# One decoder layer: the rests of every second weight piece on GpSimd until the MLP, the convolution as a side job, and new constants in the layout's clock

## The chip, the cores and the metric

The kernel runs on one core of a Trainium2 chip. The engines of the core are named as in the profile: PE (TensorE, matrix products; PEld its weight loads), DVE (VectorE), ACT (ScalarE), POOL (GpSimd) and SP (SyncE, which here issues the larger loads). The metric is the device time of the whole program in microseconds (us), as the median of several runs.

## What is computed

One inference step of one layer: 256 prompt tokens and 8 x 8 sample tokens (320 columns together), model width 2048, all in fp32. Cut to what matters:

```python
z = rmsnorm(x, g_mix) @ w_in            # 2048 x 3584: B, C, H, q, k, v, qx
y_conv = b * short_conv(c * hc, conv_w) # 3 taps along the sequence, width 512
y_swa  = sink_attention(q, k, v, ...)   # 8 heads, window 128, biases from a table
y_x    = cross_attention(qx, mk, mv)    # 4 heads, mk and mv from mem @ w_mem_k, w_mem_v
x = x + concat(y_conv, y_swa, y_x) @ w_out
x = x + square(relu(rmsnorm(x, g_mlp) @ w_up)) @ w_down   # width 8192
...
def short_conv(u_ext, w):
    length = u_ext.shape[1] - (CONV_K - 1)
    out = w[0] * u_ext[:, 0:length]
    for i in range(1, CONV_K):
        out = out + w[i] * u_ext[:, i:i + length]
    return out
```

The sample tokens attend to caches of their own (window keys and values, memory keys and values), and the new keys, values and convolution states are outputs too.

## The kernel before

**Weights.** All weight matrices are cut into 360 *pieces* of 256 x 512, 512 KB each. SP loads a piece into one of four buffers `raw`. `split_piece` then makes two halves of it in one of four buffers: ACT rounds it to fp32r (`wh`), and the *rest*, `wl = raw - wh`, is left to `rest()`, which issues the subtraction on DVE and then calls `load_piece()`: the load of the piece four places on goes into the `raw` buffer that the rest has just read. In SP's row of instructions that load waits for the rest, and everything behind it on SP waits too. The split of piece i is put out once PE has used piece i - 4. Each product is three fp32r matmuls (high by high, high by low, low by high).

**Groups and steps.** Pieces are used in this order: cross queries (0 to 7), K and V (8 to 15), w_mem_k (16 to 23), w_mem_v (24 to 31), Q (32 to 47), C (48 to 55), H (56 to 63), B (64 to 71), w_out (72 to 103), then the MLP (104 to 359). A *step* is one call of `run_unit`: 12 matmuls of 320 columns, half a piece, or 6 of 512 columns in the two memory groups. At its end `boundary()` puts out, in this order, late evacuations, evacuations (`h_evac` multiplies H by C and does the convolution; `b_evac` multiplies the convolution by B), the rests, and one step of the side jobs.

**Side jobs.** Norms, both attentions, the position biases and the convolution's state run as generators in `Side`: each is resumed at a boundary, puts out a few instructions and yields. When a job goes on is decided while the program is built, by a clock of its own, `Pace`: it adds up a cost for each operation on each engine (`cost`, `load`), and `after(...)` yields until by that clock the tiles are written. `LAG` is the landing time that it gives to loads other than weights. The order in which instructions stand in each engine's row thus follows from these numbers; on the chip each engine takes its row in order and waits on semaphores. `cross_sample` loads the cached memory keys (`cmk`) and values (`cmv`) into buffers `w`, two of a batch at a time and two batches ahead; `swa_sample` does the same with the cached window keys and values (`csk`, `csv`). `bias_sample_job` fetches the sample biases with eight small loads (`z<-sk_d`) from POOL's queue. `pre_late` copies the old window keys and values from one place of memory to another, also from POOL's queue (`old_k`, `old_v`), at the turn from B to w_out.

**Names and lines in the profile.** Nearly every operation is recorded at line 166, the wrapper in `Paced`. Weight products are `mm<-...`, those of the side jobs `ax<-...`. The convolution works on `lx` (H times C with its earlier columns) into `z`, 128 x 336.

Of the kernel before, what the change touches and what calls it, by code (L numbers as in the profile page):

```python
# [9 lines left out]
F32 = mybir.dt.float32  # L10
F32R = mybir.dt.float32r
AF = mybir.ActivationFunctionType
ALU = mybir.AluOpType
# [18 lines left out]
NEG = -1e30  # L32

NW2 = 12
LAG = 6.0
WARM = 10
C_B, C_C, C_H, C_Q, C_K, C_V, C_X = 0, 512, 1024, 1536, 2560, 2816, 3072


# [53 lines left out]
class Pace:  # L93
# [12 lines left out]
    def cost(self, eng, op, out, ins):  # L106
        n = max(a.free_size() for a in [out] + ins)
        if eng == "pe":
            n = out.free_size()
            if ins[0].dtype == F32R:  # L110
                return 0.0033 + n / 2400.0
            quarter = 0.25 if out.partition_size() == 32 else 1.0
            return 0.0009 * n if op == "transpose" else max(0.11, n / 600.0) * quarter
        if eng == "act":
            return 0.1 + n * 0.00083
        if eng == "dve":
            return 0.08 + n * 0.00104
        return 0.1 + n * 0.0025

    def issue(self, eng, op, out, ins):  # L120
# [13 lines left out]

    def load(self, out):
        start = max(self.clock["dma"], self.clock["pe"])
        self.clock["dma"] = start + out.free_size() * 4 * out.partition_size() / 330e3
        self.wrote[out.name] = (self.clock["dma"] + (2.0 if out.name.startswith("raw") else LAG), "dma")

    def ready(self, tiles):  # L140
# [6 lines left out]
class Paced:  # L147
# [3 lines left out]
    def __getattr__(self, op):  # L151
        f = getattr(self.engine, op)
        if not callable(f) or op == "preload_act_table_set":
            return f

        def issue(*args, **kw):
            aps = [a for a in list(kw.values()) + list(args) if isinstance(a, bass.AP)]
            out = kw["out"] if "out" in kw else args[0]
            if op == "dma_start":
                if out.name not in self.pace.dram:  # L160
                    self.pace.load(out)
            else:
                if "accum_out" in kw:
                    self.pace.wrote[kw["accum_out"].name] = (self.pace.clock[self.name] + 0.5, self.name)
                self.pace.issue(self.name, op, out, [a for a in aps if a is not out])
            return f(*args, **kw)  # L166

        return issue
# [79 lines left out]
def trunk_step(ctx: ExitStack, tc: tile.TileContext, I, O):  # L248
    nc = tc.nc
    pace = Pace()  # L250
    side = Side(NW2, pace)
    pace.dram = {a.name for a in list(I.values()) + list(O.values())}
    pe, act, dve = (Paced(pace, n, e) for n, e in (("pe", nc.tensor), ("act", nc.scalar), ("dve", nc.vector)))
    pool, sp = Paced(pace, "pool", nc.gpsimd), Paced(pace, "dma", nc.sync)
# [14 lines left out]
    zs = Slots(zp, "z", 10)  # L269
# [16 lines left out]
    def zt(cols=336):  # L286
        return zs.need([P, 336])
# [43 lines left out]
    def gcol(name, i=0):  # L331
        return cols[:, col[name] + i:col[name] + i + 1]
# [6 lines left out]
    st = {}  # L339
# [62 lines left out]
    def load_piece():  # L402
        i = count["load"]
        if i >= len(pieces):
            return
        count["load"] += 1
        wt[i] = raw_p.tile([P, 2, 512], F32, name="raw", tag="raw")
        if i > 1:
            load_part(i, slice(0, 2))
# [5 lines left out]
    def split_piece():  # L415
        i = count["split"]
        if i >= len(pieces) or (i >= SPL and done_at.get(i - SPL, count["unit"]) >= count["unit"]):
            return
        count["split"] += 1
        pace.clock["act"] = max(pace.clock["act"], pe_done.get(i - SPL, 0.0))  # L420
        r = wt.pop(i)
        h = wsp.tile([P, 2, 512], F32R, name="wh", tag="wh")
        l = wsp.tile([P, 2, 512], F32R, name="wl", tag="wl")
        wt[i] = (h, l)
        if i < 2:

            for c in range(2):
                k = 2 * i + c
                x = xblk[0][:, k, :]
                if k:  # L430
                    split_act(S0h[:, k, :], S0l[:, k, :], x, gcol("g_mix", k))
                else:
                    dve.tensor_scalar(out=S0h[:, k, :], in0=x, scalar1=gcol("g_mix", k), scalar2=None, op0=ALU.mult)
                    dve.scalar_tensor_tensor(out=S0l[:, k, :], in0=x, scalar=gcol("g_mix", k),
                                             in1=S0h[:, k, :].bitcast(F32), op0=ALU.mult, op1=ALU.subtract)
                act.activation(out=h[:, c, :], in_=r[:, c, :], func=AF.Copy)
                dve.tensor_tensor(out=l[:, c, :], in0=r[:, c, :], in1=h[:, c, :].bitcast(F32), op=ALU.subtract)
            side.flags.add(f"x{i}")
            load_piece()
            return  # L440
        act.activation(out=h, in_=r, func=AF.Copy)

        def rest():
            dve.tensor_tensor(out=l, in0=r, in1=h.bitcast(F32), op=ALU.subtract)
            load_piece()

        subs.append(rest)

    def add_group(w, c0, korder, a, evac, kind="std", needs=None, pre=None, k0=0):
# [36 lines left out]
    def run_unit(un):  # L486
# [6 lines left out]
        while count["split"] <= un["base"] + un["ps"][-1]:  # L493
            split_piece()
# [43 lines left out]
        if u == 2 * un["n"] - 1 or u % 2 and len(un["ps"]) == 1 or u == 3:  # L538
            for i in un["ps"]:
                done_at[un["base"] + i] = count["unit"]  # L540
                pe_done[un["base"] + i] = pace.clock["pe"]
        count["unit"] += 1
        split_piece()
        boundary()

# [13 lines left out]
    def split_act(hi, lo, src, gain):  # L559
        act.activation(out=hi, in_=src, func=AF.Copy, scale=gain)  # L560
        dve.scalar_tensor_tensor(out=lo, in0=src, scalar=gain, in1=hi.bitcast(F32), op0=ALU.mult, op1=ALU.subtract)
# [567 lines left out]
    def usample(m):  # L1129
        return st["u"][:, m, 258:UC].rearrange("p (b r) -> p b r", r=10)  # L1130

    def per_batch(a):
        return a.rearrange("p (b t) -> p b t", t=NS)
# [19 lines left out]
    def h_evac(m, ps):  # L1153
        if m == 0:
            st["y"] = {}
        u = st["u"]
        z = zs.must([P, 336])
        dve.tensor_tensor(out=z[:, 0:T], in0=ps, in1=rb, op=ALU.mult)
        dve.tensor_tensor(out=u[:, m, 2:258], in0=z[:, 0:TP], in1=u[:, m, 2:258], op=ALU.mult)
        us = usample(m)[:, :, 2:10]  # L1160
        dve.tensor_tensor(out=us, in0=per_batch(z[:, TP:T]), in1=us, op=ALU.mult)
        dve.tensor_scalar(out=z, in0=u[:, m, 0:336], scalar1=gcol("conv_w", m), scalar2=None, op0=ALU.mult)
        for i in (1, 2):
            dve.scalar_tensor_tensor(out=z, in0=u[:, m, i:i + 336], scalar=gcol("conv_w", 4 * i + m), in1=z,
                                     op0=ALU.mult, op1=ALU.add)
        st["y"][m] = z
        if m == 3:
            side.add("convout", conv_out_job())

    def conv_out_job():  # L1170
        cu = yield from zt()
        u = st["u"]
        for m in range(4):
            dve.tensor_copy(out=cu[:, m * 18:m * 18 + 2], in_=u[:, m, 256:258])
            dve.tensor_copy(out=cu[:, m * 18 + 2:m * 18 + 18].rearrange("p (b r) -> p b r", r=2),
                            in_=u[:, m, 258:UC].rearrange("p (b r) -> p b r", r=10)[:, :, 8:10])
        pool.dma_start(out=O["conv"], in_=cu[:, 0:72])
        zs.put(cu)
        lx.put(st.pop("u"))
        yield 1  # L1180

    def b_evac(m, ps):
        side.until(["cp"])
        y = st["y"][m]
        z = zs.must([P, 336])
        dve.tensor_tensor(out=z[:, 0:T], in0=ps, in1=rb, op=ALU.mult)
        dve.tensor_tensor(out=z[:, 0:TP], in0=z[:, 0:TP], in1=y[:, 0:TP], op=ALU.mult)
        dve.tensor_tensor(out=z[:, TP:T].rearrange("p (b t) -> p b t", t=NS),
                          in0=z[:, TP:T].rearrange("p (b t) -> p b t", t=NS),
                          in1=y[:, 256:336].rearrange("p (b r) -> p b r", r=10)[:, :, 2:10], op=ALU.mult)  # L1190
        act.activation(out=S1h[:, m, :], in_=z[:, 0:T], func=AF.Copy)
        zs.put(y)

        def rest():
            dve.tensor_tensor(out=S1l[:, m, :], in0=z[:, 0:T], in1=S1h[:, m, :].bitcast(F32), op=ALU.subtract)
            zs.put(z)

        later.append(rest)
        if m == 3:
            side.flags.add("conv")  # L1200
# [92 lines left out]
    add_group(w_in, C_Q + 512, order, xa, q_evac(4))  # L1293
    add_group(w_in, C_C, order, xa, c_evac)
    add_group(w_in, C_H, order, xa, h_evac)
    add_group(w_in, C_B, order, xa, b_evac)

    for g in range(4):
# [30 lines left out]
    bk = ax.must([P, 512])  # L1329
    for _ in range(WARM):  # L1330
        nc.tensor.matmul(out=bk[:, 0:P], lhsT=ones, rhs=ones, start=True, stop=True)
# [72 lines left out]
```

## Time and profile before

| | us |
|---|---|
| median of 3 runs (1320.54 to 1321.83) | 1320.77 |
| the profiled execution | 1322.82 |
| its span | 1320.7 |
| PE busy | 1311.3 |
| DVE busy | 674.7 |
| ACT busy | 541.3 |
| POOL busy | 18.1 |

The profiled execution's own time holds 2.1 us beside the span that the trace covers. POOL issues a few loads and fills a few tiles; a load that it issues counts as about half a microsecond of its time. The mean clock granted to PE is 0.997 of full speed. In the rows of a timeline the first column is the start, the second the duration in us, and a bracket holds the idle time just before the instruction and what ended it.

### The profile page before, as it was taken

What the parts mean: (1) busy time and instruction counts of PE and PEld (TensorE: products, weight loads), DVE (VectorE), ACT (ScalarE), POOL (GpSimd) and SP (SyncE); (2) the same over time, 40 slices, a digit from 0 to 9 for tenths busy, and PEclk for the clock granted to TensorE, in tenths of its full rate; (3) what the DMA queues carried; (4) which work ended last, traced back from release to release, by engine and by line L of the source; (5) the groups of instructions that cost most, each with busy time, mean ns of one, the idle gap of its engine ahead of it and who ended that gap; (6) DMA issues with size and microseconds to landing.
All of it is one profiled execution on the core that took longest, in us unless ns stands there. A gap on an engine that the chain in (4) does not pass through costs nothing.

```text
span 1320.7 us, 21556 instructions
## 1 busy us (share of the span) xinstructions
PE 1311.3 (99%) x8956; PEld 1289.5 (98%) x8956; DVE 674.7 (51%) x1025; ACT 541.3 (41%) x801; POOL 18.1 (1%) x37
## 2 busy tenths in 40 slices
PE   9999999999999999999999999999999999999999
PEld 9988999889999999999999999999999999999998
DVE  6877665766566444443344543434444344444343
ACT  7684563334355444332334433234442223443321
POOL 1011000000000000000000000000000000000000
PEclk9999999989999999999999999999999999999999
DMA  8668454456344444445444445444444444444552
GB/s 313 236 200 286 167 188 159 178 184 228 108 153 159 148 157 144 144 144 160 156 148 144 141 149 166 151 145 142 147 159 158 144 153 135 155 153 155 171 172 72
DMA packets 65489, 217.03 MB, mean 164 GB/s; under 512 B 8438, under 2 KB 10718, under 8 KB 65361
## 3 DMA queue, kind: packets, MB, share of 16 engines
q1 hardware_dynamic: 63184, 210.14, 48.1%
q0 software_dynamic: 1776, 5.26, 1.1%
q8 instruction: 70, 1.15, 0.4%
q10 hardware_dynamic: 432, 0.28, 0.1%
q14 instruction: 27, 0.21, 0.0%
HBM read 211.53 MB, written 7.65 MB: 166 GB/s over the span
## 4 chain that ended last, share of the span: by engine, by line
PE 93%; DVE 3%; DMA 2%; ACT 1%; issue 1%; SPq 0%; DVEq 0%; ACTq 0%
PE mm L166 90%; PE ax L166 3%; DMA raw<-in_w_in 2%; DVE z L166 1%; DVE wl L166 1%; ACT wh L166 1%; DVE lx L166 0%; ACT lx L166 0%; DVE S1l L166 0%; DVE w L166 0%; DVE sm L166 0%; ACT z L166 0%; ACT S0h L166 0%; DVE S0l L166 0%; ACT S1h L166 0%
## 5 line engine op out<-in xcount | busy, mean ns | idle before, releaser
L166 DVE TENSOR_TENSOR wl<-raw,wh 128x1024 fp32r<-128x1024 f32 (+1 forms) x362 | 436.1, 1217 | 487.3 <-ACT wh L166 476.4
L166 ACT ACTIVATE wh<-raw 128x1024 fp32r<-128x1024 f32 (+1 forms) x362 | 374.5, 1050 | 629.1 <-PE mm L166 581.1
L166 PE MATMUL mm<-S0h,wh 128*128 128x320 f32 x1472 | 455.8, 311 | 0.8 <-DVE z L166 0.4
L166 PE MATMUL mm<-S0h,wl 128*128 128x320 f32 x1472 | 453.6, 310 | 1.1 <-DVE wl L166 1.1
L166 PE MATMUL mm<-S0l,wh 128*128 128x320 f32 x1472 | 453.7, 310 | 0.3 <-DVE S0l L166 0.3
L166 PE MATMUL mm<-S1h,wh 128*128 128x320 f32 x1280 | 397.4, 310 | 0.0
L166 PE MATMUL mm<-S1h,wl 128*128 128x320 f32 x1280 | 395.5, 309 | 0.0
L166 PE MATMUL mm<-S1l,wh 128*128 128x320 f32 x1280 | 395.5, 309 | 0.0
L166 PEld LDWEIGHTS mm<-S0h,wh 128*128 128x128 f32 x1472 | 276.5, 188 | 3.3 <-issue 1.4
L166 PEld LDWEIGHTS mm<-S0h,wl 128*128 128x128 f32 x1472 | 276.6, 188 | 1.3 <-DVE wl L166 1.3
L166 PEld LDWEIGHTS mm<-S0l,wh 128*128 128x128 f32 x1472 | 276.7, 188 | 0.6 <-DVE S0l L166 0.6
L166 PEld LDWEIGHTS mm<-S1h,wh 128*128 128x128 f32 x1280 | 240.4, 188 | 0.2
L166 PEld LDWEIGHTS mm<-S1l,wh 128*128 128x128 f32 x1280 | 240.4, 188 | 0.2
L166 PEld LDWEIGHTS mm<-S1h,wl 128*128 128x128 f32 x1280 | 240.3, 188 | 0.0
L166 DVE TENSOR_TENSOR lx<-mm,lx 128x320 f32<-128x320 f32 (+1 forms) x97 | 46.8, 485 | 77.1 <-PE mm L166 77.0
L166 ACT ACTIVATE z<-z 128x320 f32<-128x320 f32 (+1 forms) x118 | 55.0, 470 | 64.4 <-DVE z L166 63.2
L166 DVE TENSOR_TENSOR S1l<-z,S1h 128x320 fp32r<-128x320 f32 x68 | 33.4, 491 | 51.1 <-ACT S1h L166 51.1
L166 ACT ACTIVATE S1h<-z 128x320 fp32r<-128x320 f32 x68 | 32.1, 472 | 7.5 <-DVE z L166 5.5
L166 DVE SCALAR_TENSOR_TENSOR z<-mm,r2b 128x320 f32<-128x320 f32 x64 | 31.0, 484 | 0.0
L166 PE MATMUL mm<-wh,S1h 128*128 128x512 f32 x64 | 25.6, 400 | 0.0
L166 PE MATMUL mm<-wl,S1h 128*128 128x512 f32 x64 | 25.0, 391 | 0.0
L166 PE MATMUL mm<-wh,S1l 128*128 128x512 f32 x64 | 25.0, 391 | 0.0
(162 smaller groups left out, 432.5 us busy)
## 6 DMA issues: line engine op xcount, KB each, us to landing
raw<-in_w_up SPq DMA_DIRECT2D x128, 512.0 KB, 3.3
raw<-in_w_down SPq DMA_DIRECT2D x128, 512.0 KB, 3.3
raw<-in_w_in SPq DMA_DIRECT2D x54, 512.0 KB, 4.1
raw<-in_w_out SPq DMA_DIRECT2D x32, 512.0 KB, 3.7
raw<-in_w_mem_k SPq DMA_DIRECT2D x8, 512.0 KB, 6.4
raw<-in_w_mem_v SPq DMA_DIRECT2D x8, 512.0 KB, 4.3
w<-in_cmk SPq DMA_DIRECT2D x16, 256.0 KB, 5.8
w<-in_cmv SPq DMA_DIRECT2D x16, 256.0 KB, 5.1
```

The costliest lines, as they stand in the source:

```text
L166: return f(*args, **kw)
```

## The change

Three things. First, the rests of the odd pieces from 9 to 103, 48 in all, are subtracted on POOL instead of DVE; the load behind each then waits for POOL. Second, the three operations of the convolution leave `h_evac`, which gives its buffer back; a new side job `convy` does them one tile every two steps, and adds the job of the convolution's state at its end; `b_evac` is held until `convy` is done. Third, the constants of the build-time clock are others: each operation on ACT and DVE costs 0.1 and 0.08 more, a matmul 0.01 more, loads flow at 410 instead of 330 KB per us, `LAG` is 3.5 instead of 6.0, and an operation with an accumulated output takes longer. From piece 104 on the order of all engines is as it was.

```diff
@@ -32,8 +32,9 @@
 NEG = -1e30
 
 NW2 = 12
-LAG = 6.0
+LAG = 3.5
 WARM = 10
+POOLED = 8, 104
 C_B, C_C, C_H, C_Q, C_K, C_V, C_X = 0, 512, 1024, 1536, 2560, 2816, 3072
 
 
@@ -108,13 +109,13 @@
         if eng == "pe":
             n = out.free_size()
             if ins[0].dtype == F32R:
-                return 0.0033 + n / 2400.0
+                return 0.0135 + n / 2400.0
             quarter = 0.25 if out.partition_size() == 32 else 1.0
             return 0.0009 * n if op == "transpose" else max(0.11, n / 600.0) * quarter
         if eng == "act":
-            return 0.1 + n * 0.00083
+            return 0.2 + n * 0.00084
         if eng == "dve":
-            return 0.08 + n * 0.00104
+            return 0.16 + n * 0.00105
         return 0.1 + n * 0.0025
 
     def issue(self, eng, op, out, ins):
@@ -134,7 +135,7 @@
 
     def load(self, out):
         start = max(self.clock["dma"], self.clock["pe"])
-        self.clock["dma"] = start + out.free_size() * 4 * out.partition_size() / 330e3
+        self.clock["dma"] = start + out.free_size() * 4 * out.partition_size() / 410e3
         self.wrote[out.name] = (self.clock["dma"] + (2.0 if out.name.startswith("raw") else LAG), "dma")
 
     def ready(self, tiles):
@@ -161,8 +162,10 @@
                     self.pace.load(out)
             else:
                 if "accum_out" in kw:
-                    self.pace.wrote[kw["accum_out"].name] = (self.pace.clock[self.name] + 0.5, self.name)
+                    self.pace.wrote[kw["accum_out"].name] = (self.pace.clock[self.name] + 0.9, self.name)
                 self.pace.issue(self.name, op, out, [a for a in aps if a is not out])
+                if "accum_out" in kw:
+                    self.pace.clock[self.name] += 0.19
             return f(*args, **kw)
 
         return issue
@@ -440,8 +443,10 @@
             return
         act.activation(out=h, in_=r, func=AF.Copy)
 
+        eng = pool if i % 2 and POOLED[0] <= i < POOLED[1] else dve
+
         def rest():
-            dve.tensor_tensor(out=l, in0=r, in1=h.bitcast(F32), op=ALU.subtract)
+            eng.tensor_tensor(out=l, in0=r, in1=h.bitcast(F32), op=ALU.subtract)
             load_piece()
 
         subs.append(rest)
@@ -1159,13 +1164,21 @@
         dve.tensor_tensor(out=u[:, m, 2:258], in0=z[:, 0:TP], in1=u[:, m, 2:258], op=ALU.mult)
         us = usample(m)[:, :, 2:10]
         dve.tensor_tensor(out=us, in0=per_batch(z[:, TP:T]), in1=us, op=ALU.mult)
-        dve.tensor_scalar(out=z, in0=u[:, m, 0:336], scalar1=gcol("conv_w", m), scalar2=None, op0=ALU.mult)
-        for i in (1, 2):
-            dve.scalar_tensor_tensor(out=z, in0=u[:, m, i:i + 336], scalar=gcol("conv_w", 4 * i + m), in1=z,
-                                     op0=ALU.mult, op1=ALU.add)
-        st["y"][m] = z
+        zs.put(z)
         if m == 3:
-            side.add("convout", conv_out_job())
+            side.add("convy", conv_job())
+
+    def conv_job():
+        u = st["u"]
+        for m in range(4):
+            z = yield from zt()
+            dve.tensor_scalar(out=z, in0=u[:, m, 0:336], scalar1=gcol("conv_w", m), scalar2=None, op0=ALU.mult)
+            for i in (1, 2):
+                dve.scalar_tensor_tensor(out=z, in0=u[:, m, i:i + 336], scalar=gcol("conv_w", 4 * i + m), in1=z,
+                                         op0=ALU.mult, op1=ALU.add)
+            st["y"][m] = z
+            yield 2
+        side.add("convout", conv_out_job())
 
     def conv_out_job():
         cu = yield from zt()
@@ -1180,7 +1193,7 @@
         yield 1
 
     def b_evac(m, ps):
-        side.until(["cp"])
+        side.until(["cp", "convy"])
         y = st["y"][m]
         z = zs.must([P, 336])
         dve.tensor_tensor(out=z[:, 0:T], in0=ps, in1=rb, op=ALU.mult)
```

The first place is the end of group H in DVE's row, before: the evacuations of tiles 1, 2 and 3 (`z<-mm,rb` is an H tile scaled from PE's sums, `lx` its product with C, the last two rows of each the convolution), with the sample attention's softmax between.

```order
L166 TENSOR_TENSOR z_2893<-mm,rb 128x320
L166 TENSOR_TENSOR lx_1381<-z_2893,lx_1381 128x256
L166 TENSOR_TENSOR lx_1381<-z_2893,lx_1381 128x8x8
L166 TENSOR_SCALAR z_2893<-lx_1381,cols 128x336
L166 SCALAR_TENSOR_TENSOR z_2893<-lx_1381,cols,z_2893 128x336 x2
L166 TENSOR_TENSOR z_2918<-mm,rb 128x320
L166 TENSOR_TENSOR lx_1381<-z_2918,lx_1381 128x256
L166 TENSOR_TENSOR lx_1381<-z_2918,lx_1381 128x8x8
L166 TENSOR_SCALAR z_2918<-lx_1381,cols 128x336
L166 SCALAR_TENSOR_TENSOR z_2918<-lx_1381,cols,z_2918 128x336 x2
```

The same place in DVE's row now, from tile 2 of H to the first convolved tile, past the turn to group B:

```order
L169 TENSOR_TENSOR z_3029<-mm,rb 128x320
L169 TENSOR_TENSOR lx_1384<-z_3029,lx_1384 128x256
L169 TENSOR_TENSOR lx_1384<-z_3029,lx_1384 128x8x8
L169 TENSOR_TENSOR z_3052<-mm,rb 128x320
L169 TENSOR_TENSOR lx_1384<-z_3052,lx_1384 128x256
L169 TENSOR_TENSOR lx_1384<-z_3052,lx_1384 128x8x8
L169 TENSOR_TENSOR wl<-raw,wh 128x1024
L169 TENSOR_SCALAR z_3059<-lx_1384,cols 128x336
L169 SCALAR_TENSOR_TENSOR z_3059<-lx_1384,cols,z_3059 128x336 x2
```

The convolution's rows stand behind the last H evacuation and a rest, one tile at a time.

The second place is POOL's row from the start to the sample biases, before (`gkx` a gain vector; `rv_d`, `sk_d` position biases on their way through memory):

```order
L166 DMA gkx<-in_g_k_x 128x128
L166 MEMSET w_5_441 128x512
L166 MEMSET w_6_442 128x512
L166 DMA rv_d<-w_12_539 8x384
L166 DMA sk_d<-rv_d 1024x1x384
L166 DMA z_1093<-sk_d 8x136 x8
```

And now:

```order
L169 DMA gkx<-in_g_k_x 128x128
L169 ISA
L169 TENSOR_TENSOR wl<-raw,wh 128x1024 [waits DMAHW4_49,PE_49,Activation_49]
L169 MEMSET w_6_455 128x512
L169 MEMSET w_7_456 128x512
L169 DMA rv_d<-w_9_461 8x384 [waits Activation_49]
L169 DMA sk_d<-rv_d 1024x1x384 [waits DMASW6_49]
```

The `ISA` row reloads POOL's library of instructions; the first rest, that of piece 9, follows it. Seven more rests follow behind these rows, and then the eight bias loads with rests right behind them.

The third place is SP's row around the first cached keys of the cross attention (group w_mem_k), before, with the semaphores that each waits for (`DVE_49`: the rest):

```order
L166 DMA raw<-in_w_mem_v 128x1024 [waits DMAHW5_49,DVE_49]
L166 DMA w_17_1090<-in_c_own 128x2x64
L166 DMA w_17_1090<-in_c_rep 32x128
L166 DMA w_18_1102<-in_cmk 128x512
L166 DMA w_19_1104<-in_cmk 128x512
L166 DMA w_20_1106<-in_cmk 128x512 [waits DMAHW6_49]
L166 DMA w_21_1108<-in_cmk 128x512 [waits DMAHW7_49]
```

And now:

```order
L169 DMA w_17_1037<-in_c_own 128x2x64
L169 DMA w_17_1037<-in_c_rep 32x128
L169 DMA raw<-in_w_mem_v 128x1024 [waits DMAHW4_49,Pool_49]
L169 DMA w_18_1079<-in_cmk 128x512
L169 DMA w_19_1081<-in_cmk 128x512
L169 DMA w_20_1083<-in_cmk 128x512 [waits DMAHW5_49]
L169 DMA w_21_1085<-in_cmk 128x512 [waits DMAHW6_49]
```

A weight load has come between the two small loads and the keys, and it waits for a rest on POOL. The keys are put out five steps ahead of their first use, the bias loads on POOL seven. At the first cached window keys (group C) it is the same now:

```order
L169 DMA raw<-in_w_in 128x1024 [waits DMAHW7_49,DMAHW3_49,Pool_49]
L169 DMA w_71_2541<-in_csk 128x512 [waits DMAHW4_49,PE_49]
L169 DMA w_72_2543<-in_csv 128x512 [waits DMAHW5_49,PE_49]
L169 DMA w_73_2545<-in_csk 128x512 [waits PE_49]
```

Before, the weight load ahead of `csk` there waited for DVE (`[waits DMAHW6_49,DMAHW2_49,DVE_49]`). The use of the first key stands four steps behind its load now.

## Prediction

> **What bounds the kernel now.** I read the busy table and the slices first, for which engine fills the span, then the chain, the waits and one stretch in windows of 5 us.
>
> ```profile
> PE 1311.3 (99%) x8956; PEld 1289.5 (98%) x8956; DVE 674.7 (51%) x1025; ACT 541.3 (41%) x801; POOL 18.1 (1%) x37
> PEclk9999999989999999999999999999999999999999
> PE 93%; DVE 3%; DMA 2%; ACT 1%; issue 1%; SPq 0%; DVEq 0%; ACTq 0%
> 423.36 894.08 PE mm L166 x6096
> ```
>
> PE is busy 99% of the span and carries 93% of the chain. From 423 us on the chain is nothing but matmuls, 894.08 / 6096 = 0.1467 us each, 3.52 us for a piece's 24. The order is unchanged from the MLP on (piece 104) and the matmuls are the same ones, so nothing can come from there. What is to be had is PE's idle time and lost clock ahead of 423 us. The list of waits gives the first:
>
> ```profile
> PE ax L166 <- DVE z L166: 2.6, 2, 1.9
> PE mm L166 <- DVE wl L166: 1.1, 1, 1.1
> PE mm L166 <- DVE z L166: 0.4, 1, 0.4
> PE ax L166 <- ACT z L166: 0.2, 1, 0.2
> ```
>
> These are sums, counts and longest waits. PE's timeline puts them in place, the wait in brackets:
>
> ```profile
> 39.42 0.41 PE L166 MATMUL ax<-z,mean_d 128*128 128x320 f32 x1 [0.17 <-ACT z L166]
> 40.48 0.42 PE L166 MATMUL ax<-z,mean_d 128*128 128x320 f32 x1 [0.64 <-DVE z L166]
> 256.68 0.41 PE L166 MATMUL mm<-S0h,wh 128*128 128x320 f32 x1 [0.45 <-DVE z L166]
> 260.05 0.42 PE L166 MATMUL mm<-S0h,wl 128*128 128x320 f32 x1 [1.06 <-DVE wl L166]
> 274.98 0.79 PE L166 MATMUL ax<-vns,z 64*128 64x128 f32 x2 [1.95 <-DVE z L166]
> ```
>
> Three of the five lie at the turn from group H to group B, 0.45 + 1.06 + 1.95 = 3.46 us. The windows there give busy time of PE, PEld, DVE, ACT, POOL, then the granted clock and DMA's share:
>
> ```profile
> 250.00:255.00 5.00, 5.00 (x37) 4.99 (x37) 4.72 (x12) 2.42 (x8) 0.00 (x0) 1.00 0.02 3
> 260.00:265.00 5.00, 4.95 (x38) 4.44 (x39) 4.69 (x24) 1.57 (x4) 1.71 (x3) 1.00 1.02 344
> 270.00:275.00 5.00, 3.06 (x27) 2.47 (x25) 2.41 (x8) 2.44 (x4) 0.00 (x0) 0.97 0.87 297
> 275.00:280.00 5.00, 5.00 (x29) 3.78 (x30) 1.66 (x4) 0.55 (x2) 0.00 (x0) 0.50 0.70 220
> 280.00:285.00 5.00, 5.00 (x33) 5.00 (x32) 0.88 (x1) 1.06 (x1) 0.00 (x0) 0.85 0.01 3
> ```
>
> DVE is full, then DMA, then PE stands; behind the 1.95 us wait PE runs "busy" at half clock. Lost by the clock: 5 x (0.03 + 0.50 + 0.15) = 3.4 us. The 1.06 us wait brought no such drop, so on this trace the point lies between 1.06 and 1.95. How DVE gets to PE there is told by the chain:
>
> ```profile
> 258.78 1.22 DVE wl L166
> 261.75 9.58 DMA raw<-in_w_in
> 271.43 1.07 ACT wh L166
> 272.52 1.23 DVE wl L166
> ```
>
> A late rest delays the load queued behind it; that load takes 9.58 us beside the two cache copies, and the split of its piece follows. The place costs 3.46 + 3.4 = **6.9 us**, the two waits near 40 us 0.81, together 7.7: all that this change can win.
>
> **The change, part by part.**
>
> ```profile
> L166 DVE TENSOR_TENSOR wl<-raw,wh 128x1024 fp32r<-128x1024 f32 x358 | 433.4, 1223 | 487.3 <-ACT wh L166 476.4 <-DMA w<-in_cmk 5.6 <-DMA raw<-in_w_in 2.3
> L166 DVE SCALAR_TENSOR_TENSOR z<-lx,cols,z 128x336 f32<-128x336 f32 x8 | 4.6, 569 | 0.3
> L166 DVE TENSOR_SCALAR z<-lx,cols 128x336 f32<-128x336 f32 x4 | 1.6, 396 | 0.1
> ```
>
> *Convolution spread.* Per tile, 0.396 + 2 x 0.569 = 1.53 us leave each H evacuation, 6.1 us in all, most of it from 245 to 259 us; they return one tile at a time in group B, where the window at 275 us has DVE busy 1.66 of 5. *Rests moved.* 48 rests x 1.223 = 58.7 us leave DVE before piece 104; in the 15 us ahead of 260 two of them. So 1.53 x 4 + 2.4 = 8.5 us go from a stretch in which DVE was late by about 1.1: I take the whole place as removed, -6.9. It could return only by the cache copies, which now meet loads issued earlier. The waits near 40 us: DVE loses work there and the planner's new costs move the step; -0.8, bound by 0.
>
> *What a rest costs on POOL.* No row shows such an operation. The nearest are POOL's fills:
>
> ```profile
> L166 POOL MEMSET w<- 128x512 f32 x6 | 3.0, 540 | 55.7 <-PE ax L166 55.7
> 29.15 0.53 POOL L166 DMA_DIRECT2D gkx<-in_g_k_x  x1
> 88.48 4.02 POOL L166 DMA_DIRECT2D z<-sk_d  x8 [43.43 <-ACT wh L166]
> ```
>
> A fill of 128 x 1024 is 2 x 0.54 = 1.1 us with no stream read; a rest reads two and writes one, so up to three times that, 3.2. Between 1.1 and 3.2 I take the middle, 2.2: 1.0 above DVE. POOL has two pieces' time, 7.04 us, between two of its rests, so its own load is no bound. [...]
>
> *Startup.* POOL's first rest (piece 9) stands behind a library reload.
>
> ```profile
> 1.19 1.28 ACT L303 ACT_TABLE_LOAD   x1 [1.19 <-PEq L1391]
> w<-in_cmk SPq DMA_DIRECT2D x8, 256.0 KB, 5.7
> 36.75 0.31 PE L166 MATMUL mm<-S0h,wl 128*128 128x320 f32 x1
> ```
>
> The fetch of gkx ends at 29.68; with a reload like ACT's 1.28 (the nearest row) the rest can go at 31.3 when wh is there, ends at 33.5, and PE first wants it at 36.75: cost 0. It is free up to 36.75 - 2.2 - 29.68 = 4.9. If a reload is instead as long as a fetch from memory of 256 KB takes to land, 5.7 in the second row, it costs 0.8: bounds 0 to 0.8, value 0. Nothing below 0, since PE does not wait there today. [...] No trace here shows a reload.
>
> *Loads behind POOL's rests.* SP issues in order: a weight load waits for its rest, and cache loads stand behind it. Two places are tight.
>
> ```profile
> 91.73 1.91 SPq L166 DMA_DIRECT2D w<-in_cmk  x4
> 98.26 0.39 PE L166 MATMUL mm<-wl,S1h 128*128 128x512 f32 x1
> 98.49 0.39 PE L166 MATMUL mm<-wh,S1l 128*128 128x512 f32 x1
> 98.81 1.07 PE L166 MATMUL ax<-w,w 128*32 128x256 f32 x16
> w<-in_csk SPq DMA_DIRECT2D x4, 256.0 KB, 4.7
> ```
>
> First, the cross keys of batch 0. Today they are issued at 91.73 and used at 98.81, 7.1 us later, without a wait. Now eight bias fetches (4.02 us) stand on POOL ahead of a rest (2.2), and a weight load and then the four key loads stand on SP behind it: start of the fetches + 4.0 + 2.2 + 0.5 for issuing the weight load + 1.4 to the fourth key load (1.91 / 4 an issue) = 8.1. Landing takes 5.7 by these keys' own median and 4.7 by that of the window's keys (the row of csk): 12.8 to 13.8. PE uses them seven steps after the fetches; a step is six matmuls, 0.23 us from start to start (98.26 to 98.49), 1.38, so 9.7, and with four normalizing matmuls of about 0.2 some 10.5. The stall is 2.3 to 3.3, less what POOL does ahead of its step, since its fetches wait for a buffer alone: value 2.0, bounds 0.5 to 3.3.
>
> ```profile
> 227.94 0.36 SPq L166 DMA_DIRECT2D w<-in_csk  x1
> 236.62 0.43 PE L166 MATMUL ax<-w,qs 128*32 128x128 f32 x8
> L166 ACT ACTIVATE wh<-raw 128x1024 fp32r<-128x1024 f32 x358 | 371.9, 1055 | 627.2 <-PE mm L166 581.1 <-issue 33.9 <-DMA raw<-in_w_in 7.7
> ```
>
> Second, the window's keys. Today 8.7 us pass from issue to use. Now the load is issued in the step of an odd piece: ACT's split 1.05, POOL's rest 2.2, weight load 0.5, landing 4.7 = 8.45; the use is four steps of 1.76 later, 7.04. Stall 1.4, and the second key, two issues later, makes it up to 2.7: value 1.7, bounds 0.4 to 2.7. At the other cache loads the same count leaves 0 to 1.6 us spare: 0, at most 1 in all.
>
> *Planner's constants.* They cost nothing by themselves; their moves are in the terms above.
>
> The sum, against this execution (span 1320.7, its own time 1322.82, and 2.05 above the runs' median 1320.77, so span and median agree to 0.1): 1320.77 - 6.9 - 0.8 + 0 + 2.0 + 1.7 + 0.5 (half of that last 1) = **1317.3**.
>
> **Rivals.**
>
> *All gain, no new wait.* If POOL's rests take nearer 1.1 and the loads land in time: 1320.77 - 7.7 = 1313.1. For it: today's margins; against it: the two counts above, which miss even then, by 1.2 and 0.3.
>
> *One new wait trips the clock.* At 1.95 us the trace pays 3.4 more, at 1.06 nothing; 2.0 is on the edge. Then 1317.3 + 3.4 = 1320.7: no change. [...]
>
> *Slower: cache loads held behind POOL's rests.* The same mechanism at both places past 1.95 us. It decides where a rest on POOL takes some 2.5: the waits are then 2.3 and 2.0, and 1317.3 + 0.6 + 2 x 3.4 = 1324.7; at the upper bounds 3.3 and 2.7 it is 1320.77 - 7.7 + 0.5 + 6.0 + 6.8 = 1326.4. For it: LAG falls from 6.0 to 3.5 while the rows show keys landing in 4.7 and 5.7.
>
> *DVE and POOL get in each other's way.*
>
> ```profile
> 60.00:80.00 20.00, 19.95 (x107) 17.35 (x106) 17.11 (x33) 15.00 (x32) 0.00 (x0) 1.00 0.48 154
> ```
>
> In these 20 us of the w_mem_k group, the fullest that pooled rests fill, lie about 3.5 of them. If DVE stands while POOL works, each costs it 2.2 - 1.22 = 1.0 instead of freeing it: 17.11 + 3.5 = 20.6 of 20, late by 0.6; at 3.2 a rest 24.0, late by 4. That gives 1317.9 to 1321.3, likeliest 1319.5, and with a clock drop behind it up to 1324.7. [...]
>
> *It does not do what it says:* the copies collide again and half of the place stays: 1320.77.
>
> **How the numbers follow.** The forecast (1315.5 to 1318.5) has 0.37, all gain 0.13, one clock drop 0.20, both 0.12, interference 0.12, the place staying 0.06. 0.2% is 2.64 us, about what a measurement of this kernel can tell from no change: faster is below 1318.13, slower above 1323.41. Faster: all gain and 0.35 of the forecast, 0.48. Slower: both drops, a third of interference (with a drop), half of the staying place (the new waits on top of it), 0.12 + 0.04 + 0.03 = 0.19. Same: the rest, 0.33. The range runs from 1313.0, just under all gain, to 1324.7, both drops at their value; what lies beyond is about 0.1 above and 0.05 below. The unknown costs (a rest of 1.1 to 3.2, the reload) lie inside through the waits that they make.
>
> **What would show it.** In the profile after: no PE wait and clock 1.00 between 250 and 285 us (the place); DVE below 4.0 of 5 there (spread); a group of POOL rests with a mean near 2.2, and DVE's rests still at 1.22 (over 1.5 would be interference); a PE wait for a cache load at the cross keys near 98 us and at the window's keys near 235, each 1 to 2.5 us, with or without a window at clock 0.5 behind it; POOL's first rest ending before 36.75. Wrong would be the sum if POOL's rests exceed 3, if PE waits for `wl` from POOL anywhere, or if the stretch after 260 us still has loads of over 8 us that PE waits for.

## The result: 1.4% slower, and where the profile after shows it

The changed kernel takes 1339.82 us (median of 4 runs, 1338.91 to 1342.69) against 1321.3 of the kernel before beside it: ratio 1.0139, 95% interval 1.0116 to 1.0162. That is about 18 us slower, outside the range and on the other side of the forecast. The profiled execution's span is 1340.8, 20.1 us above that of before.

The page of after: the busy table, the clock by slices and the chain.

```profile
PE 1315.4 (98%) x8956; PEld 1292.4 (96%) x8956; DVE 663.0 (49%) x977; ACT 541.3 (40%) x801; POOL 139.0 (10%) x85
PEclk9999899999999999999999999999999999999999
PE 87%; DVE 1%; issue 1%; DMA 0%; ACT 0%; DVEq 0%
```

PE is busy 4.1 us longer with the same matmuls, the clock lost to it (below), and idle 25.4 us instead of 9.4. DVE lost 48 rests, 58.7 us of work, but its busy time fell by only 11.7. PE's waits in after, as totals, counts and longest:

```profile
PE ax L169 <- DVE w L169: 7.8, 2, 4.4
PE ax L169 <- DVE z L169: 4.6, 5, 1.8
PE ax L169 <- DMA w<-in_c_hot: 4.5, 1, 4.5
PE ax L169 <- DMA w<-in_csk: 2.2, 2, 1.1
PE mm L169 <- DVE S0l L169: 0.9, 1, 0.9
PE ax L169 <- DMA w<-in_cmk: 0.7, 2, 0.5
```

All but one of the new waits are those of side jobs (`ax`): the main stream has its weights in time. The largest in PE's timeline of after:

```profile
32.70 1.44 PE L169 MATMUL ax<-w,z 33*8 33x384 f32 x2 [4.52 <-DMA w<-in_c_hot]
101.56 0.41 PE L169 MATMUL ax<-z,mean_h 128*128 128x320 f32 x1 [1.77 <-DVE z L169]
139.96 1.94 PE L169 MATMUL ax<-w,w 128*32 128x128 f32 x32 [4.40 <-DVE w L169]
225.45 0.41 PE L169 MATMUL ax<-z,mean_h 128*128 128x320 f32 x1 [1.12 <-DVE z L169]
301.41 0.62 PE L169 MATMUL ax<-ident,w 128*128 128x128 f32 x2 [3.40 <-DVE w L169]
```

Windows of after around the first and the last of them (busy PE, PEld, DVE, ACT, POOL, then clock and DMA):

```profile
30.00:35.00 5.00, 2.30 (x5) 1.05 (x6) 3.76 (x6) 4.17 (x6) 1.82 (x2) 0.68 0.72 257
35.00:40.00 5.00, 5.00 (x24) 5.00 (x24) 3.66 (x6) 1.26 (x4) 2.13 (x4) 0.64 0.65 209
...
295.00:300.00 5.00, 3.02 (x21) 2.75 (x19) 4.86 (x7) 3.30 (x12) 2.42 (x1) 1.00 0.00 0
300.00:305.00 5.00, 3.59 (x15) 3.62 (x16) 4.67 (x23) 0.38 (x1) 0.56 (x1) 0.66 0.61 217
```

The wait for the hot table (the bias job's load, 4.52) and the clock behind it, 5 x (0.32 + 0.36) = 3.4, make 7.9 us. Those at 140 and 301 us make, with lost clock of 3.4 and 1.7 by the same count, 12.9. The old place at the turn from H to B is gone; the third of these stands a little behind it.

What the rests do on POOL is seen by laying DVE's timeline of after beside POOL's (start, duration):

```profile
222.65 2.39 POOL L169 TENSOR_TENSOR wl<-raw,wh 128x1024 fp32r<-128x1024 f32 x1 [5.83 <-ACT wh L169]
222.97 2.43 DVE L169 TENSOR_TENSOR z<-z,z 128x320 fp32r<-128x320 f32 x1 [1.72 <-ACT z L169]
278.88 3.42 POOL L169 TENSOR_TENSOR wl<-raw,wh 128x1024 fp32r<-128x1024 f32 x1 [6.85 <-ACT wh L169]
279.96 2.52 DVE L169 TENSOR_SCALAR z<-lx,cols 128x336 f32<-128x336 f32 x1
295.60 2.42 POOL L169 TENSOR_TENSOR wl<-raw,wh 128x1024 fp32r<-128x1024 f32 x1 [4.13 <-ACT wh L169]
295.77 2.26 DVE L169 TENSOR_TENSOR sm<-skb,sm 128x2 f32<-128x2 f32 x1
416.09 2.51 POOL L169 TENSOR_TENSOR wl<-raw,wh 128x1024 fp32r<-128x1024 f32 x1 [2.06 <-ACT wh L169]
416.74 0.49 DVE L169 TENSOR_TENSOR lx<-mm,lx 128x320 f32<-128x320 f32 x1 [0.42 <-PE mm L169]
...
333.04 3.01 POOL L169 TENSOR_TENSOR wl<-raw,wh 128x1024 fp32r<-128x1024 f32 x1 [5.40 <-ACT wh L169]
334.41 0.69 DVE L169 TENSOR_REDUCE sm<-w 128x2 f32<-128x512 f32 x1
```

The first pair shows the mechanism. `z<-z,z` starts 0.3 us after a rest on POOL and ends 0.4 us behind its end (it takes 0.48 us alone); PE's normalizing matmul at 225.45 follows at once, 1.12 us late. A subtraction of two columns takes 2.26 us instead of 0.16. The last two pairs are the exceptions: with one input from PSUM (`mm`) DVE works through a rest at its usual 0.49, and so does a reduction, with one input in all, at 0.69. In the other direction POOL's rest at 278.88, which started while DVE's own rest was running, took 3.42 instead of 2.40. One input is no sure way out: the `TENSOR_SCALAR` at 279.96, with one tile and a column of constants, took 2.52 us beside that rest and 0.38 at 299.09, and copies from SBUF are held too (2.56 us at 137.16, below). What on POOL holds them is tested below.

### The profile page after: what moved, and what is told of

Same layout as the page of the kernel before. It is cut to its first block, busy times and chain, and to the rows that moved or that the text cites. A ratio compares the mean times of both kernels' runs of the same rounds, so it can differ in the third digit from the quotient of the medians.

```text
span 1340.8 us, 21564 instructions
## 1 busy us (share of the span) xinstructions
PE 1315.4 (98%) x8956; PEld 1292.4 (96%) x8956; DVE 663.0 (49%) x977; ACT 541.3 (40%) x801; POOL 139.0 (10%) x85
## 4 chain that ended last, share of the span: by engine, by line
PE 87%; DVE 1%; issue 1%; DMA 0%; ACT 0%; DVEq 0%
PE mm L169 84%; PE ax L169 3%; DVE z L169 1%; DMA w<-in_csk 0%; DVE wl L169 0%; DVE sm L169 0%; DVE w L169 0%; ACT z L169 0%; ACT wh L169 0%; DVE lx L169 0%; DVEq L1413 0%
## 5 line engine op out<-in xcount | busy, mean ns | idle before, releaser
L169 DVE TENSOR_TENSOR wl<-raw,wh 128x1024 fp32r<-128x1024 f32 (+1 forms) x314 | 380.6, 1224 | 476.1 <-ACT wh L169 475.2
L169 POOL TENSOR_TENSOR wl<-raw,wh 128x1024 fp32r<-128x1024 f32 x48 | 120.8, 2517 | 249.5 <-ACT wh L169 232.1
```

## The experiments

Theory **P**: rests on POOL hold DVE up, and DVE hands that on to PE. Theory **C**: the new constants put uses ahead of their data. Ratios are to the kernel before on the same chip, with intervals; a microsecond figure worked out from a ratio takes 1320.8 us as the time before.

### One part at a time

Rests alone:

```diff
+        eng = pool if i % 2 and POOLED[0] <= i < POOLED[1] else dve
...
-            dve.tensor_tensor(out=l, in0=r, in1=h.bitcast(F32), op=ALU.subtract)
+            eng.tensor_tensor(out=l, in0=r, in1=h.bitcast(F32), op=ALU.subtract)
```

> The kernel before with the rests of odd pieces 9 to 103 on POOL and nothing else. Theory P (POOL's rests hold DVE up for as long as they run, and DVE hands that on to PE): DVE rows that meet a rest on POOL are about 2 us longer, DVE's busy time falls by much less than the 58 us of its 48 rests, PE waits for DVE, time 1326 to 1336. Theory C (the new constants of the layout's clock put uses ahead of their data): the old constants leave the uses where they were, PE has few new waits, time 1316 to 1322.

Measured 1335.98, ratio 1.0119 (1.0103 to 1.0136): P's range. DVE's busy time is 665.7 where 616 would be left without the 48 rests.

The constants alone, with the diff's changes to `Pace`, `Paced` and `LAG` and nothing else:

> The kernel before with the new constants of the layout's clock and nothing else. Theory C: PE waits again 4 to 5 us for the hot table in the first 40 us and 1 us each for cached keys, the clock drops behind the long one, time 1328 to 1336. Theory P: at most the waits for loads that are short, no DVE row stretched, time 1318 to 1324.

Measured 1328.38, ratio 1.0063 (1.0042 to 1.0083): C's range too. The wait is there with no rest on POOL:

```profile
31.92 0.80 PE L168 MATMUL ax<-w,z 33*8 33x384 f32 x2 [4.47 <-DMA w<-in_c_hot]
```

In PE's timeline 212 matmuls stand ahead of the hot table's before and 164 now: 48 matmuls of 0.147 us, 7 us earlier, while its load still starts near 27.5 us. So both theories hold, each for its own part.

The convolution alone, with the edits of `h_evac`, `conv_job` and `b_evac`:

> The kernel before with the convolution as a side job and nothing else. Both theories: the waits at the turn from H to B (3.5 us) and the dropped clock behind them (3.4 us) go, time 1313 to 1316. If the place depends on the rests, it stays at 1320 to 1322.

Measured 1316.4, ratio 0.997 (0.996 to 0.998), span 1314.6: 0.4 above the expected range, and faster than both kernels. The windows of this run at the place of the old waits:

```profile
250.00:255.00 5.00, 5.00 (x39) 4.99 (x37) 4.72 (x17) 2.50 (x5) 0.00 (x0) 1.00 0.01 3
255.00:260.00 5.00, 5.00 (x41) 4.49 (x40) 4.76 (x14) 1.83 (x5) 0.00 (x0) 1.00 0.56 183
...
270.00:275.00 5.00, 5.00 (x40) 4.49 (x39) 3.12 (x12) 1.61 (x3) 1.72 (x3) 1.00 1.02 325
275.00:280.00 5.00, 5.00 (x36) 4.94 (x35) 1.52 (x3) 1.06 (x1) 0.00 (x0) 1.00 0.58 220
```

PE is busy throughout at full clock. DVE is as full as before, but ends its burst without making a rest late.

Convolution and constants, all rests on DVE (`POOLED = 8, 8` in the changed kernel):

> The changed kernel with all rests back on DVE, so the convolution as a side job and the new constants. Theory P: without rests on POOL nothing holds DVE, time 1313 to 1322. Theory C: the waits for loads stay, above all that for the hot table near 32 us, time 1326 to 1334.

Measured 1335.01, ratio 1.0107 (1.0086 to 1.0128): above even C's range. The hot table is waited for 4.70 us, and another wait stands in w_out:

```profile
361.11 2.00 PE L169 MATMUL ax<-ident,w 128*128 128x128 f32 x8 [4.45 <-DVE w L169]
```

Here no POOL is at work. DVE was merely busy from 350.5 to 361 with three softmax steps, evacuations and two rests, and the layout had put their use too early. That speaks for C, and against my picture of P as the larger part.

### What on POOL holds DVE

The kernel before, every rest on DVE, with work of no use added on POOL behind each odd rest; `dmy` is a tile of 128 x 224. Reads:

```diff
+            if i % 2 and 8 <= i < 104:
+                for q in range(4):
+                    a = h[:, :, q * 112:(q + 1) * 112].bitcast(F32)
+                    nc.gpsimd.tensor_tensor(out=dmy, in0=a, in1=a, op=ALU.subtract)
```

> The kernel before, every rest still on DVE and the order unchanged, with work added on POOL at the places of the 48 odd pieces: four subtractions of 128x224 that read two fp32 streams of wh from SBUF and whose result nobody uses (some 2.1 us together). Theory P (a POOL instruction that reads SBUF holds a DVE instruction with two inputs from SBUF until it ends): such DVE rows are stretched by up to one POOL instruction, about 0.5 us, rows with an input from PSUM are not; time 1322 to 1332. If DVE is late for another reason (the rests' length on POOL, the order), 1319.5 to 1321.5.

Fills:

```diff
+            if i % 2 and 8 <= i < 104:
+                nc.gpsimd.tensor_tensor(out=dmy[0:1, 0, 0:8], in0=h[0:1, 0, 0:8].bitcast(F32),
+                                        in1=h[0:1, 0, 0:8].bitcast(F32), op=ALU.subtract)
+                for q in range(8):
+                    nc.gpsimd.memset(dmy, 0.0)
```

> As the run with added reads, but with eight fills of 128x224 on POOL that read nothing (some 2 us together, behind one tiny reading instruction that sets their time). Theory P with reads as the cause: no DVE row stretched beyond 0.1 us, time 1319.5 to 1321.5. If any work of POOL holds DVE: as much as with reads, 1322 to 1332.

Reads: 1343.78, ratio 1.0173 (1.0158 to 1.0188). Fills: 1336.01, ratio 1.0116 (1.0101 to 1.0131). Groups of both runs (count, busy time, mean in ns), reads first:

```profile
L449 POOL TENSOR_TENSOR dmy<-wh 128x224 f32<-128x224 f32 x192 | 160.1, 834 | 208.3 <-ACT wh L166 196.6
L166 DVE SCALAR_TENSOR_TENSOR S1l<-w,cols,S1h 128x256 fp32r<-128x256 f32 x16 | 10.5, 665 | 2.5 <-ACT S1h L166 2.5
```

```profile
L450 POOL MEMSET dmy<- 128x224 f32 x384 | 110.7, 288 | 22.2
L166 DVE SCALAR_TENSOR_TENSOR S1l<-w,cols,S1h 128x256 fp32r<-128x256 f32 x16 | 7.5, 477 | 2.5 <-ACT S1h L166 2.5
```

Reads stretch DVE's row from 477 to 665 ns on average, and DVE's busy time from 674.7 to 705.2. Fills leave every row alone: 675.6 in all, and no DVE rest above 1.23 us. So in these two runs it is POOL's reads, and not its being at work, that hold DVE.

The times of both runs are misses: I expected at most 1332 us with the reads and no change with the fills, and they cost 23 and 15 us. Neither time is the price of what POOL does, because the edit also changed a wait. In both runs POOL is a further reader of `wh`, and the same split on ACT then waits for PE (before, fills, reads):

```profile
59.18 1.06 ACT L166 ACTIVATE wh<-raw 128x1024 fp32r<-128x1024 f32 x1 [0.94 <-DMA raw<-in_w_mem_k]
65.00 1.06 ACT L166 ACTIVATE wh<-raw 128x1024 fp32r<-128x1024 f32 x1 [6.88 <-PE mm L166]
68.45 1.06 ACT L166 ACTIVATE wh<-raw 128x1024 fp32r<-128x1024 f32 x1 [5.17 <-PE mm L166]
```

Counted in the traces, PE has ended 340 weight matmuls at this split before, and 377 in both runs; at the next two splits it is 387 and 394 before, 396 and 420 in both runs. The same counts at different times are a wait that stands in the program, not a load that comes late. PE's wait of 3.97 us at 69.96 in the run with fills follows from it. Why a further reader moves the wait is not tested. Only the difference of the two runs, 7.5 us (1.0173 against 1.0116), can be put down to what POOL reads.

### The same order, other engine

Rests on POOL in the order of before: the layout's clock still counts them on DVE.

```diff
-            dve.tensor_tensor(out=l, in0=r, in1=h.bitcast(F32), op=ALU.subtract)
+            if i % 2 and 8 <= i < 104:
+                pace.issue("dve", "tensor_tensor", l, [r, h.bitcast(F32)])
+                nc.gpsimd.tensor_tensor(out=l, in0=r, in1=h.bitcast(F32), op=ALU.subtract)
+            else:
+                dve.tensor_tensor(out=l, in0=r, in1=h.bitcast(F32), op=ALU.subtract)
```

> The kernel before with the rests of odd pieces 9 to 103 issued on POOL, while the layout's clock still counts them on DVE, so that every engine's order is as before except for the rests. Theory P: DVE rows held as in the run of the rests alone (DVE busy some 45 us above 616), time 1326 to 1338. If the cost came from the other order that the planner made with POOL's costs: 1313 to 1320.

Measured 1334.02, ratio 1.0099 (1.0082 to 1.0116). DVE's busy time is 679.4, above that of before though 48 rests have left it: it is held for 63 us. The cost is not the planner's. The split that waits for PE's 377th weight matmul in the last two runs starts here after 348, so this run has not their further wait.

The converse, the changed kernel's order with the rests back on DVE:

```diff
-            eng.tensor_tensor(out=l, in0=r, in1=h.bitcast(F32), op=ALU.subtract)
+            if eng is pool:
+                pace.issue("pool", "tensor_tensor", l, [r, h.bitcast(F32)])
+                nc.vector.tensor_tensor(out=l, in0=r, in1=h.bitcast(F32), op=ALU.subtract)
+            else:
+                eng.tensor_tensor(out=l, in0=r, in1=h.bitcast(F32), op=ALU.subtract)
```

> The changed kernel with its 48 rests back on DVE, while the layout's clock still counts them on POOL: every engine's order is that of the changed kernel, only the rests change engine. Theory P (rests on POOL hold DVE): the waits of PE for DVE at 69, 98, 102, 225 and 301 us and the clock lost at 301 go (4.6 + 3.4 + 1.7 us), that at 140 us (4.4 + 3.4) goes if POOL held it up; the wait for the hot table stays at about 4.5 with 3.4 of clock; time 1322 to 1331. If the order alone makes the waits: 1336 to 1341, or more, since DVE has 59 us more to do.

Measured 1328.1, ratio 1.0054 (1.0039 to 1.0069). PE's waits for DVE at 69, 98, 102, 225 and 301 us are gone; of those that are left, three in PE's timeline:

```profile
32.88 1.44 PE L169 MATMUL ax<-w,z 33*8 33x384 f32 x2 [5.21 <-DMA w<-in_c_hot]
110.17 0.62 PE L169 MATMUL ax<-w,w 128*32 128x256 f32 x4 [1.65 <-DMA w<-in_cmk]
135.47 1.08 PE L169 MATMUL ax<-w,w 128*32 128x128 f32 x32 [0.80 <-DVE w L169]
```

The wait at 140 us shrank from 4.40 to 0.80. SP's and DVE's rows of after show why it was long, and those of this run (second fence) why it is short:

```profile
121.66 11.69 SPq L169 DMA_DIRECT2D raw<-in_w_in  x4
133.44 0.38 SPq L169 DMA_DIRECT2D w<-in_cconv  x1
137.16 2.56 DVE L169 COPY lx<-w 128x16 f32<-128x16 f32 x4 [3.97 <-DMA w<-in_cconv]
```

```profile
121.76 7.49 SPq L169 DMA_DIRECT2D raw<-in_w_in  x4
129.35 0.38 SPq L169 DMA_DIRECT2D w<-in_cconv  x1
134.81 0.41 DVE L169 COPY lx<-w 128x16 f32<-128x16 f32 x4 [2.52 <-DMA w<-in_cconv]
```

The cached convolution rows stood on SP behind four weight loads that wait for rests, 4.1 us longer in after; DVE waited for them with its row full behind it; and the copies that use them were held once more, 2.56 instead of 0.41, by the rest at 137.18. Both ways of a POOL rest to be late, its own length and its hold on DVE, add up here. How the 11 us between this run and the changed kernel split between the two is not separated.

### The constants

LAG back to 6.0, the other new constants kept:

> The kernel before with the new constants except LAG, which stays at 6.0. Theory LAG (3.5 is too short for the loads it stands for): the wait for the hot table falls from 4.5 to below 1 us, no dropped clock, 1317 to 1322. Theory costs (the old costs let PE's clock run behind and so gave every wait a margin that the exact ones lack): the wait stays above 3 us, 1326 to 1329. In PE's order the first use of the hot table stands 24 matmuls later than with 3.5 and 24 earlier than before, so a wait of about 1 us is what I expect.

The wait for the hot table is 1.06 us, as expected; the time is not: 1338.62, ratio 1.0133 (1.0118 to 1.0148), above the ranges of both theories. The old turn from H to B, with the convolution in one piece, now also holds up cached keys, which then meet the two cache copies:

```profile
266.34 0.66 PE L168 MATMUL ax<-w,qs 128*32 128x128 f32 x8 [6.75 <-DMA w<-in_csk]
```

So this run doesn't tell costs from LAG, and the next two set each of them alone on the kernel with the spread convolution.

> The kernel before with the convolution spread and LAG 3.5, the old costs. Theory LAG (3.5 is too short): waits for the hot table and for cached keys of several us, 1322 to 1330. Theory costs (the old costs give the margin): the hot table's step stands where it stood in PE's order (24 and 24 matmuls later than with the new constants), no wait for it, at most 1 to 2 us for cached keys: 1315 to 1320.

> The kernel before with the convolution spread and the new costs, LAG 6.0. Theory LAG: near the convolution alone, 1315 to 1318. Theory costs: about 1 us for the hot table, which stands 24 matmuls earlier than before, and further waits of PE for DVE and ACT that the old costs kept away: 1319 to 1330.

LAG alone: 1321.88, ratio 1.0003 (0.9993 to 1.0013). Costs alone: 1328.21, ratio 1.0053 (1.0035 to 1.0071). Both stand beside the convolution alone at 0.997, and both together (above) at 1.0107. Over the convolution alone that is 4.4 us for LAG, 11.0 for the costs, 18.1 for both. The costs alone came out as the theory of costs had it; LAG alone came out 2 us above that theory's range and just under the other's, so LAG has a price of its own. The first two rows are from the run with LAG, the others from that with the costs:

```profile
107.43 0.63 PE L166 MATMUL ax<-w,w 128*32 128x256 f32 x4 [1.19 <-DMA w<-in_cmk]
128.79 1.08 PE L166 MATMUL ax<-w,w 128*32 128x128 f32 x32 [1.20 <-DVE w L166]
```

```profile
33.58 0.80 PE L168 MATMUL ax<-w,z 33*8 33x384 f32 x2 [1.56 <-DMA w<-in_c_hot]
284.26 1.17 PE L168 MATMUL ax<-ident,w 128*128 128x128 f32 x4 [2.75 <-DVE w L168]
```

The old cost of a 320-column matmul was 0.0033 + 320 / 2400 = 0.137 us, 7% below the 0.147 of the trace. PE's planned clock therefore ran behind, each wait for "written by now" took more steps than the chip needed, and that was the margin. The exact cost takes it away, and so do the shorter landing time and the faster loads. This is my reading of the code: the new costs were not set one by one, and those of ACT and DVE, which rose too, work the other way.

### Taking the largest wait out of the changed kernel

Both tables of the bias job loaded at the program's start, the layout's clock told as before, and all other order unchanged:

```diff
+    early = zs.must([P, 336]), w2.must([P, 512])
+    nc.vector.memset(early[0][0:33, 0:8], 1.0)
+    nc.gpsimd.dma_start(out=early[0][0:32, 0:8], in_=I["rel_bias_table"])
+    nc.gpsimd.dma_start(out=early[1][0:33, 0:384], in_=I["c_hot"])
...
-        pool.dma_start(out=hot[0:33, 0:384], in_=I["c_hot"])
+        pace.load(hot[0:33, 0:384])
```

> The changed kernel, with the hot table and the bias table loaded at the program's start; every engine's order else as in the changed kernel, the rests on POOL. The wait of 4.5 us at 32.7 us and the 3.4 us of clock behind it go, all else stays: 1330 to 1334. If the wait is only handed on to the next thing that was late: 1336 to 1340.

The wait goes and nothing is won: 1342.63, ratio 1.0166 (1.0149 to 1.0183), above the range for a wait handed on. It is handed on 15 us down the same row:

```profile
48.13 1.00 PE L169 MATMUL ax<-z,mean_d 128*128 128x320 f32 x2 [3.65 <-ACT z L169]
```

While PE stood for the hot table, ACT and DVE could catch up with the norm of the inputs; without the pause PE comes to that norm too early. (That reading is from the order of the waits; nothing else was changed to test it.) The same edit with the rests on DVE:

> The changed kernel with both edits: rests on DVE in the changed order, hot table loaded at the start. What is left is the changed order with exact constants and the convolution spread: 1314 to 1323, the remaining waits those for cached keys (about 3 us together) and, if it was not POOL's, that at 140 us.

Measured 1326.22, ratio 1.0039 (1.0027 to 1.0052): 2.0 us less than with the table late, with intervals that overlap, and not the 8 of the wait and its clock; above the expected range. In PE's timeline of this run the cached keys are waited for longer, and the clock falls behind them (3.4 us):

```profile
107.21 0.64 PE L169 MATMUL ax<-w,w 128*32 128x256 f32 x4 [1.95 <-DMA w<-in_cmk]
109.07 1.07 PE L169 MATMUL ax<-w,w 128*32 128x256 f32 x4 [1.22 <-DMA w<-in_cmk]
```

## Why the prediction was wrong

*The place at the turn from H to B, -6.9.* Right in mechanism, with a smaller size. The convolution alone removes it whole: the span falls by 6.1 us, the median by 4.0 (ratio 0.997). It needed no rest moved. The size was read from one execution with a granted clock of 0.997, 2.05 us above the median, and taken off the median. That the span of this execution equals the median of the runs' own times is chance, since an execution's own time holds 2.1 us beside its span. Not every execution of the kernel before loses the 3.4 us of clock: beside the last two runs one took 1318.59 us at a clock of 1.000 and another 1322.46 at 0.997.

*The waits near 40 us, -0.8.* They are absent in after, which stood still for 4.5 us just ahead.

*A rest on POOL, 2.2 us.* 2.40 undisturbed, mean 2.52:

```profile
L169 POOL TENSOR_TENSOR wl<-raw,wh 128x1024 fp32r<-128x1024 f32 x48 | 120.8, 2517 | 249.5 <-ACT wh L169 232.1 <-PE ax L169 17.4
```

*The reload at the start, 0.* Right: the first rest starts at 33.33 when ACT's split is done, ends at 35.7, and PE never waits for it. No row of the trace shows the reload itself; it fits into the 3.18 us for which POOL had been idle, from the end of gkx's issue at 30.15, and the longer one that the prediction weighed (5.7 us, 0.8 of cost) would not have.

*Loads behind rests, 2.0 and 1.7.* At the cross keys 0.7, at the window's keys 2.2 in two waits, together a little less than forecast. The one that mattered more, the cached convolution rows at 140 us (7.8 with its clock), I did not count.

*"Planner's constants. They cost nothing by themselves."* **This is the step that failed first.** With the convolution spread they cost 18 us where the planner counts all rests on DVE (1.0107 against 0.997), and in the changed kernel's own order, rests on DVE, 11 (1.0054). I had read the order for the moves of loads, not for how far each use had moved towards its data: the hot table's matmul, 48 places earlier, stood in the same rows of PE, and 48 x 0.147 = 7 us against a load that lands no earlier can be worked out without a run.

*DVE and POOL in each other's way.* The rival was the second mechanism; the sum left it out, and **its price was mis-sized**. I counted DVE's load per 20 us and found it late by 0.6 to 4. What counts is the single step: a row of 0.2 to 0.5 us that PE is about to use becomes 2.5, and of the 58.7 us that left DVE's queue, 47 come back as holding (663.0 against 616). In the changed order the rests on POOL cost 11 us (1.0139 against 1.0054), in the order of before 13 (1.0099). The sign I had named, DVE's rests above 1.5 us, would have missed it: their mean stayed at 1.224, and the rows that stood were others.

*The clock.* The three longest waits in after (4.52, 4.40 and 3.40 us) took 3.4, 3.4 and 1.7 us on top, as the forecast's rival had it: 8.5 us in after, 3.4 before.

Of the 20.1 us of span, PE's waits make 16.0 and the clock 5.1 (differences of after and before), less 1.0 that the records do not place. By the ratios, the spread convolution gives -4.0, the changed order of the constants and of a planner that counts rests on POOL 11.1, and the rests themselves on POOL 11.2: 18.3 of the 18.4 us. Another order of the steps gives other shares: the rests alone cost 16 us, and the early hot table shows that a wait taken out can come back elsewhere.

## What to carry to other kernels

Before moving elementwise work to POOL, see what DVE does meanwhile: here rows of 0.16 and 0.48 us with both operands in SBUF took 2.26 and 2.43 us beside a rest of 2.4 us on POOL. The offload bought time only beside rows that did not stand (a row with an operand in PSUM at its 0.49 us, a reduction at its 0.69), and its price was paid in latency at the next hand-over to PE (1.12 us at 225.45, 3.40 at 301.41), not in DVE's load, which fell from 674.7 to 663.0 us. A layout made by a planner may be good because its costs are wrong: here nearer ones, as I read it, removed a hidden margin, so keep one on purpose, and compare the distance of each load to its use in the old and new order. Try parts alone: here one of three gave all of the gain (1316.4 us) and the other two each cost more than that.

## What was not expected of the hardware

The clock's drop has no plain threshold in the length of one wait in these traces: 1.77 us at 101.56 in after brought none, 1.56 us at 45.40 in the run with both edits cost 1.7, and 2.75 with 0.69 behind it some 3.4 in the run with the new costs. What is lost comes in pieces: in windows of 5 and 10 us, each drop in these traces comes to about 1.7 us or twice that (1.7 with the constants alone, 3.4 before, 3.4, 3.4 and 1.7 in after). In windows of 1 us the last drop in after is a clock of 0.74, 0.50, 0.50 and 0.56 from 301 to 305 us, so half the clock for 3.4 us; that of the kernel before is 0.50 in each window from 275 to 281 us, with 0.84 ahead and 0.75 behind, so half the clock for 6.8 us. What decides whether a wait of 1.5 to 2 us brings a drop stays open here.
